# A bidirectional encoder layer: four staging tiles for streamed rows, and a transposed channel tile that stays in its accumulator

## The chip, the cores and the metric

The kernel runs on one core of a Trainium2 chip. The metric is the device time of one execution in microseconds (us); lower is better. The core's engines each run their own list of instructions in order: TensorE (PE) for matmuls and transposes, with its weight loads as a second row in the profile (PEld), VectorE (DVE), ScalarE (ACT) and GpSimd (POOL) for elementwise work, and SyncE (SP), which here only issues transfers (DMAs) from HBM to SBUF. POOL and ACT issue some DMAs too. Semaphores order the engines among each other.

## The reference

One layer over two batches with the same weights: a prompt P of 512 tokens and a sample S of 1024 tokens, 1024 channels. Cut to what matters here:

```python
proj = group_rmsnorm(h, norm_mix_pre) @ w_in
y_ssd, y_hy = ...                 # chunked state-space scan; long convolution
mix = concatenate([y_ssd, y_hy]) @ w_out            # 2048 -> 1024
h = h + group_rmsnorm(mix, norm_mix_post)
u = group_rmsnorm(h, norm_ffn_pre)
ff = (silu(u @ w_gate) * (u @ w_up)) @ w_down       # hidden width 2816
h = h + group_rmsnorm(ff, norm_ffn_post)
gate = sigmoid(group_rmsnorm(h, ple_norm_pre) @ w_ple_gate)
e = p_l @ w_ple_proj                                # 256 -> 1024
h = h + group_rmsnorm(gate * e, ple_norm_post)
```

All inputs and outputs are float32.

## The kernel before

**Matmuls.** Each float32 operand is split into a high part and a low part of a reduced format (`fp32r`): ACT copies with rounding (`split_ps`, L325), DVE or POOL subtracts (L326, L293). `mm3` (L301 to L303) then makes three matmuls: high by high, and the two mixed ones. Weights are loaded by SP into `wst` (L277) and split into `whi` and `wlo`.

**The end of the program**, from about 1640 us, is where the change acts; `build` writes it at L1441 and following. First P ends its FFN. Then S is done in two groups of 512 tokens:

- the out-projection of group 0 (`out_group`), its first half of 512 output channels together with P's post-FFN chain, then P's embedding gate (`ple`), then the second half;
- the out-projection of group 1 in two halves, with the normalisation chain of group 0 (`out_post`) between its steps; after it the chain of group 1 on its own (`rush`);
- S's embedding projection (`ple_proj`), whose results are stored in HBM as `e_s`;
- gate and up projections (`gate_up`), whose products are stored in HBM as `hid_s`;
- the down projection of both groups (`down_group`), with the post-FFN chain of group 0 in the steps of group 1;
- the embedding gates and the outputs.

**Streamed rows.** The out-projection (16 rows of 128 channels) and the down projection (22 rows) don't hold their left operand in SBUF. For each half, `streamed` loads one row of 128 channels x 512 tokens into a staging tile `mx` (SP, L1196; from `mix_s` or `hid_s`, 256 KB), and `split_ps` makes `mh` (ACT) and `ml` (DVE) of it. There are two `mx`, three `mh` and three `ml`. A load into a tile that was used before waits until the DVE subtraction has read it. `stream_gemm` takes two rows a step, for four token tiles: 2 x 4 x 3 = 24 matmuls of 128 x 512.

`mx` has other users. In `ple_proj` for S it holds the two loads of embedding rows per group (L1352, transposed at L1356) and eight evicted tiles per group (ACT, L1370), each stored to `e_s` at the following line. In the first job of `gate_up` it holds the sums of weights that DVE makes (L1227).

**The chains.** `post_steps` is a generator: for each of four token tiles of an accumulator `acc` it normalises (DVE, L1059), adds the residual row `t` (loaded by SP at L1050, added by DVE at L1060), normalises again back into `acc[t]` (L333), transposes it 128 x 128 at a time into a PSUM bank (L339), and splits the result. Two residual rows are loaded at the chain's start, the other two on the way. In `half`, one step of the chain is taken after each step of the matmuls.

**The channels of S.** For S's FFN the split goes by `Sums.take` instead. The gate and up projections there use a seven-product scheme for a 2 x 2 block matrix, so the tiles of tokens 0 and 1 are held until those of tokens 2 and 3 are there, and seven combinations of them are made and split (`bh`, `bl`). In the kernel before, ACT copies the transposed tile from PSUM to one of two tiles `stage` (L129), each 128 x 4 x 128. The tokens are taken in the order 0, 2, 1, 3, so that a held tile is used by the next token tile.

**Order.** The order on each engine is set by the framework when the program is built: it simulates the instructions by its own cost model and lists them by that, and the tile pools say when a tile comes free. A change in the number of tiles can so move instructions that the change does not name. `rush` and `post` run with raised priority.

Of the kernel before, what the change touches and what calls it, by code (L numbers as in the profile page):

```python
# [112 lines left out]
class Sums:  # L113
# [8 lines left out]
    def block(self, p):  # L122
        return [x[p - 1] for x in self.parts]

    def take(self, ps, k, t):
        K, nc = self.k, self.k.nc
        if t < 2:
            x = self.stage[t, k] = K.T(self.pool, [128, 4, 128], "stage")
            nc.scalar.activation(x, ps, AF.Copy)  # L129
            return  # L130
        c = slice((t - 2) * 128, (t - 1) * 128)

        def put(p, x):
            K.split_ps(x, *[z[:, :, c] for z in self.block(p)])

        def diff(out, a, b):
            nc.vector.tensor_tensor(out=out, in0=a, in1=b, op=ALU.subtract)

        b11, b21 = self.stage[t - 2, 0], self.stage[t - 2, 4]
        if k == 0:  # L140
            w = self.stage[t, 0] = K.T(self.pool, [128, 4, 128], "wsum")
            diff(w, ps, b11)
            put(1, b11)
            put(5, w)
            return
        w = self.stage[t, 0]
        put(3, ps)
        diff(w, ps, w)
        put(2, b21)
        put(6, w)  # L150
        diff(b11, w, b11)
        put(7, b11)
        diff(b21, b21, w)
        put(4, b21)
# [12 lines left out]
class Kern:  # L167
# [160 lines left out]
    def norm_tile(self, pool, src, dst, gain, u, t, wide=False, r=None):  # L328

        nc = self.nc  # L330
        if r is None:
            r = self.rstd(self.sumsq(pool, src), D)
        nc.vector.scalar_tensor_tensor(dst, src, r, gain, ALU.mult, ALU.mult)  # L333
        n = 8 if wide else 4
        for k in range(0, 8, n):
            ps = self.gps().rearrange("p a (k n) -> p (a k) n", k=4) if wide else \
                self.aps().rearrange("p (k n) -> p k n", k=4)
            for i in range(n):
                nc.tensor.transpose(ps[:, i], dst[:, (k + i) * 128:(k + i + 1) * 128], self.ident)  # L339
            if isinstance(u, Sums):  # L340
                u.take(ps, k, t)
            else:
                self.split_ps(ps, *u.put(k, n, t))

# [1052 lines left out]
    def build(self):  # L1397
# [40 lines left out]
        def tags(pool, *sizes):  # L1438
            return {t: (pool, t, n) for t, n in sizes}

        with self.pool("mix_s", side="right") as mp, ExitStack() as right:  # L1441
            pm = tags(mp, ("mx", 2), ("mh", 3), ("ml", 3))
            tr = right.enter_context(self.pool("out_s", side="right"))
            po = pm | tags(tr, ("acc", 4), ("row", 2), ("t4", 2), ("junk", 1), ("stage", 2), ("wsum", 1))
            with self.pool("tail_u") as tu, self.pool("tail_p") as tp:
                pl = tags(tu, ("et", 3), ("hh", 4), ("hl", 4), ("t4", 2), ("uh", 2), ("ul", 2))
                pl |= tags(tp, ("acc", 4), ("mst", 1), ("row", 2), ("junk", 1))
                pl["mx"] = pl["t4"]
                pl["ga"] = pl["acc"]
                mix = self.mix_in(P, 0, pl, 0, 8)  # L1450
                acc = self.new_acc(pl)
                self.outproj(P, 0, pl, acc, 0, mix)
                emb = self.ple_proj(pl, P, 0)
                next(emb)
                u = self.outproj(P, 0, pl, acc, 8, self.mix_in(P, 0, pl, 8, 8), lambda: self.new_u(pl, 4))
                next(emb)
                self.dma_lo = True
                u, chain = self.ffn(P, 0, pl, u)
                self.dma_lo = False
                acc = self.new_acc(po)  # L1460
                out = self.out_group(S, 0, po, acc)
                self.half(out, chain)
                self.ple_post(P, 0, pl, self.ple(P, 0, pl, u))
            self.apool = self.pools["x"][0]
            self.half(out)
            with self.pool("blocks") as tb:
                pb = pm | tags(tb, ("bh", 14), ("bl", 14))
                po |= pb
                u0, chain = self.out_post(S, 0, po, acc)
                acc = self.new_acc(po)  # L1470
                out = self.out_group(S, 1, po, acc)
                self.half(out, chain)
                self.half(out, chain)
                u1, chain = self.out_post(S, 1, po, acc)
                self.rush(chain)
                right.close()
                with self.pool("hid_s", side="right") as tr:
                    ph = pb | tags(tr, ("wsum", 3), ("sc", 5), ("gt", 6))
                    pe = pb | {"wsum": pm["mx"], "gt": pm["mh"], "sc": pm["ml"]}
                    pe |= {"et": pm["mx"], "hh": pm["mh"], "hl": pm["ml"]}  # L1480
                    self.apool = self.pools["m"][0]
                    for g in range(2):
                        for _ in self.ple_proj(pe, S, g):
                            pass
                    both = {0: u0, 1: u1}
                    self.gate_up(S, [(p, m, {g: both[g] for g in gs}) for p, gs, ms in (
                        (pe, [0], (0,)), (ph, [1], (0,)), (ph, [0, 1], range(2, NF, 2))) for m in ms], pe)
                with self.pool("end_s", side="right") as tr:
                    pe = pb | tags(tr, ("row", 3), ("t4", 3), ("junk", 1), ("mst", 2))
                    pe |= {"acc": pe["bl"], "ga": pe["bh"]}  # L1490
                    self.wide_tail = True
                    v0, chain = self.down_group(S, 0, pe)
                    v1, chain = self.down_group(S, 1, pe, chain)
                    self.rush(chain)
                    for g, v in ((0, v0), (1, v1)):
                        self.ple_post(S, g, pe, self.ple(S, g, pe, v))
# [30 lines left out]
```

## Time and profile before

| | |
|---|---|
| runs | 2855.67, 2855.22, 2851.17 us; median 2855.22 |
| profiled execution | 2852.23 us, span 2850.3 us |
| PE busy | 2683.8 us, 94% of the span |
| DVE, ACT, POOL busy | 1742.6, 1336.4, 1380.7 us |

How to read it: a row of groups gives line, engine, operation, destination<-sources, shape, count, then the busy time and the mean of one in ns, and then the idle time just ahead of these instructions with what ended it. A row of waits gives the engine and line that waited, what it waited for, the total in us, how often, and the longest. "SPq" is SP's DMA queue: the instruction at its head waits. PEclk is the clock that PE was granted, as a share of the full one. In the chain of waits each row has a start, a length and what took it.

### The profile page before, as it was taken

The page shows a single profiled execution, that of the slowest core. Times are in us where ns is not written, and L with a number is a line of the kernel's source. Part 1 is how long each engine was busy: PE and PEld are TensorE (multiplying, and loading weights), DVE is VectorE, ACT ScalarE, POOL GpSimd, SP SyncE. Part 2 cuts the span into 40 slices and gives each one's busy share as a digit, 9 for nine tenths or more (in the row PEclk, how much of TensorE's full clock was granted, in tenths as well). Part 3 has the DMA queues.
Part 4 walks back from the last instruction along what each step waited for, and adds up shares of the span by engine and source line. Part 5 has one row for each costly group of instructions (what it writes and reads, how often), then busy time and mean ns, then how long its engine had stood idle before and what let it go on. Part 6 is the DMA issues. An engine that isn't in the chain of part 4 may idle for free.

```text
span 2850.3 us, 41685 instructions
## 1 busy us (share of the span) xinstructions
PE 2683.8 (94%) x14696; PEld 2254.9 (79%) x14696; DVE 1742.6 (61%) x2893; ACT 1336.4 (47%) x2580; POOL 1380.7 (48%) x1137
## 2 busy tenths in 40 slices
PE   7999999999999989889999998987799999999998
PEld 5987888778888767578778776766699999877776
DVE  6767896977666896966676734475343444325345
ACT  4434445773234564745444454365533333344453
POOL 4445555443453556535444444554454444445464
PEclk9999999999999999989999999999999999999999
DMA  5544555744345576778888886565632222366665
GB/s 169 180 137 127 150 174 185 219 141 138 99 123 160 154 249 202 223 206 206 199 181 204 187 218 218 177 222 183 157 100 82 79 75 86 119 207 207 203 202 186
DMA packets 448507, 480.04 MB, mean 168 GB/s; under 512 B 29409, under 2 KB 330281, under 8 KB 445995
## 3 DMA queue, kind: packets, MB, share of 16 engines
q1 hardware_dynamic: 340923, 347.34, 40.0%
q0 software_dynamic: 28224, 68.17, 10.8%
q10 hardware_dynamic: 79152, 61.88, 6.9%
q8 instruction: 116, 1.90, 0.3%
q14 instruction: 92, 0.75, 0.1%
HBM read 346.54 MB, written 91.95 MB: 154 GB/s over the span
## 4 chain that ended last, share of the span: by engine, by line
PE 66%; DVE 15%; DMA 8%; issue 5%; POOL 3%; ACT 2%; SPq 0%; POOLq 0%; ACTq 0%; DVEq 0%
PE g L301 17%; PE g L303 16%; PE g L302 16%; PE a L302 3%; PE a L303 3%; PE a L301 3%; PE a L700 1%; DVE b L692 1%; DVE W L619 1%; DVE E L615 1%; PE a L973 1%; POOL wlo L293 1%; DMA wlo<-wst 1%; PE a L404 1%; DMA mx<-mix_s 1%
## 5 line engine op out<-in xcount | busy, mean ns | idle before, releaser
L293 POOL TENSOR_TENSOR wlo<-wst,whi 128x512 fp32r<-128x512 f32 (+1 forms) x544 | 786.1, 1452 | 756.6 <-ACT whi L292 691.5
L292 ACT ACTIVATE whi<-wst 128x512 fp32r<-128x512 f32 (+1 forms) x544 | 339.5, 628 | 532.9 <-PE g L302 330.0
L301 PE MATMUL g<-uh,whi 128*128 128x512 f32 (+1 forms) x1232 | 493.5, 401 | 8.5 <-DVE cv L393 4.4
L303 PE MATMUL g<-uh,wlo 128*128 128x512 f32 (+1 forms) x1232 | 491.6, 399 | 0.0
L302 PE MATMUL g<-ul,whi 128*128 128x512 f32 (+1 forms) x1232 | 490.9, 398 | 0.0
L301 PE MATMUL g<-bh,whi 128*128 128x256 f32 x1056 | 293.0, 283 | 14.3 <-ACT sc L1266 3.8
L303 PE MATMUL g<-bh,wlo 128*128 128x256 f32 x1056 | 294.0, 281 | 4.2 <-DMA wlo<-mx 2.7
L302 PE MATMUL g<-bl,whi 128*128 128x256 f32 x1056 | 294.3, 280 | 0.0
L301 PEld LDWEIGHTS g<-uh,whi 128*128 128x128 f32 x1232 | 233.2, 189 | 67.5 <-issue 10.4
L303 PEld LDWEIGHTS g<-uh,wlo 128*128 128x128 f32 x1232 | 232.6, 189 | 53.9 <-issue 5.8
L302 PEld LDWEIGHTS g<-ul,whi 128*128 128x128 f32 x1232 | 232.9, 189 | 53.4 <-issue 7.2
L326 DVE TENSOR_TENSOR ml<-mx,mh 128x512 fp32r<-128x512 f32 x152 | 122.4, 808 | 222.0 <-ACT mh L325 221.9
L285 POOL DMA_DIRECT2D wlo<-wst x144 | 126.0, 930 | 226.2 <-ACT wlo L284 211.1
L393 DVE SCALAR_TENSOR_TENSOR cv<-g,cols,cv 128x510 f32<-128x510 f32 (+3 forms) x192 | 193.0, 1006 | 64.9 <-ACT cv L387 62.8
L301 PEld LDWEIGHTS g<-bh,whi 128*128 128x128 f32 x1056 | 197.2, 189 | 20.0 <-DVE gt L1227 6.1
L303 PEld LDWEIGHTS g<-bh,wlo 128*128 128x128 f32 x1056 | 199.6, 189 | 4.9 <-DMA wlo<-mx 2.9
L302 PEld LDWEIGHTS g<-bl,whi 128*128 128x128 f32 x1056 | 199.5, 189 | 0.1
L301 PE MATMUL g<-whi,mh 128*128 128x512 f32 x412 | 169.7, 412 | 23.7 <-ACT mh L325 16.3
L302 PE MATMUL g<-wlo,uh 128*128 128x264 f32 (+1 forms) x576 | 191.3, 332 | 0.5 <-POOL wlo L293 0.5
L303 PE MATMUL g<-whi,ul 128*128 128x264 f32 (+1 forms) x576 | 189.9, 331 | 1.6 <-DVE rs_t L308 1.6
L309 POOL TENSOR_TENSOR rs_t<-rs_t,nhalf 128x1 f32<-128x1 f32 (+2 forms) x112 | 120.0, 1074 | 144.0 <-DVE rs_t L308 141.5
L301 PE MATMUL g<-whi,uh 128*128 128x264 f32 (+1 forms) x576 | 189.0, 330 | 0.0
(334 smaller groups left out, 6030.5 us busy)
## 6 DMA issues: line engine op xcount, KB each, us to landing
wst<-in_w_in SPq DMA_DIRECT2D x192, 256.0 KB
wlo<-wst POOLq DMA_DIRECT2D x144, 256.0 KB, 4.9
wst<-in_w_down SPq DMA_DIRECT2D x132, 256.0 KB
wst<-in_w_out SPq DMA_DIRECT2D x96, 256.0 KB
wst<-in_w_gate SPq DMA_DIRECT2D x92, 256.0 KB
wst<-in_w_up SPq DMA_DIRECT2D x92, 256.0 KB
mx<-hid_s SPq DMA_DIRECT2D x88, 256.0 KB
rw<-rows_s SPq DMA_DIRECT2D x32, 512.0 KB
```

Of the source, the lines that this page charges most:

```text
L285: nc.gpsimd.dma_start(lo, w, accum_op=ALU.add)
L292: nc.scalar.activation(hi, w, AF.Copy)
L293: (eng or nc.gpsimd).tensor_tensor(out=lo, in0=w, in1=hi.bitcast(F32), op=ALU.subtract)
L301: nc.tensor.matmul(ps, lh, rh, start=first, stop=False, skip_group_check=shared)
L302: nc.tensor.matmul(ps, lh, rl, start=False, stop=False, skip_group_check=shared)
L303: nc.tensor.matmul(ps, ll, rh, start=False, stop=last, skip_group_check=shared)
L309: nc.gpsimd.tensor_tensor(out=t[:, :w], in0=t[:, :w], in1=self.nhalf[:, :w], op=ALU.pow)
L326: self.nc.vector.tensor_tensor(out=lo, in0=ps, in1=hi.bitcast(F32), op=ALU.subtract)
L393: nc.vector.scalar_tensor_tensor(out[:, a:b], ps[:, a + d:b + d], wcol(w), out[:, a:b], ALU.mult, ALU.add)
L404: nc.tensor.transpose(ps[:, j * 128:(j + 1) * 128], srcs[i + j], self.ident)
L615: nc.vector.scalar_tensor_tensor(E[:, h], rw[:, 0, h], dbf[:, c, gh:gh + 1], rw[:, 1, h], ALU.add, ALU.min)
L619: nc.vector.scalar_tensor_tensor(W[:, h], su, dt[:, c, gh:gh + 1], W[:, h], ALU.mult, ALU.add)
```

## The change

`mx` gets four tiles in place of two (L1442), and the pool `stage` goes (L1444). With the two stages left out, the SBUF used is the same: two tiles of 128 x 512 float32 less and two more. `Sums.take` is given the source tile `dst`, that is `acc[t]`, and for tokens 0 and 1 ACT copies the transposed tile back into the 512 columns of `acc[t]` from which it came. The later differences and splits read and overwrite it there. No other line changes, and the number of instructions on each engine is the same.

```diff
-    def take(self, ps, k, t):
+    def take(self, ps, k, t, src):
+
         K, nc = self.k, self.k.nc
         if t < 2:
-            x = self.stage[t, k] = K.T(self.pool, [128, 4, 128], "stage")
+            x = self.stage[t, k] = src[:, k * 128:(k + 4) * 128].rearrange("p (k n) -> p k n", k=4)
             nc.scalar.activation(x, ps, AF.Copy)
             return
...
             if isinstance(u, Sums):
-                u.take(ps, k, t)
+                u.take(ps, k, t, dst)
...
-            pm = tags(mp, ("mx", 2), ("mh", 3), ("ml", 3))
+            pm = tags(mp, ("mx", 4), ("mh", 3), ("ml", 3))
...
-            po = pm | tags(tr, ("acc", 4), ("row", 2), ("t4", 2), ("junk", 1), ("stage", 2), ("wsum", 1))
+            po = pm | tags(tr, ("acc", 4), ("row", 2), ("t4", 2), ("junk", 1), ("wsum", 1))
```

The order before S's first out-projection is as it was; from there it differs. After the change line numbers from L125 on are one higher. In the rows below, a number behind a name tells one tile from another.

First place, term (f): SP's queue late in `gate_up`, with the first loads of the down projection's rows (`mx` from `hid_s`) among the weight loads. Before:

```order
L277 DMA wst_20916<-in_w_gate 128x4x128
L1196 DMA mx_24285<-hid_s 128x512
L277 DMA wst_20918<-in_w_gate 128x4x128
L277 DMA wst_21141<-in_w_up 128x4x128
L277 DMA wst_21143<-in_w_up 128x4x128
L277 DMA wst_21145<-in_w_up 128x4x128
L277 DMA wst_21147<-in_w_up 128x4x128
L277 DMA wst_21370<-in_w_gate 128x4x128
```

After the change, at the same place:

```order
L278 DMA wst_20908<-in_w_gate 128x4x128
L1197 DMA mx_24277<-hid_s 128x512
L1197 DMA mx_24283<-hid_s 128x512
L278 DMA wst_20910<-in_w_gate 128x4x128
L278 DMA wst_21133<-in_w_up 128x4x128
L278 DMA wst_21135<-in_w_up 128x4x128
L278 DMA wst_21137<-in_w_up 128x4x128
L278 DMA wst_21139<-in_w_up 128x4x128
L278 DMA wst_21362<-in_w_gate 128x4x128
L278 DMA wst_21364<-in_w_gate 128x4x128
L278 DMA wst_21366<-in_w_gate 128x4x128
L1197 DMA mx_24325<-hid_s 128x512
```

A second and a third row are moved here, ahead of weight loads that they stood behind.

Second place, term (b): PE in the first half of S's first out-projection (`g` is its PSUM), with the transposes of P's post-FFN chain (`a`). Before:

```order
L303 MATMUL g_16329<-whi_16629,ml_16618 128x512
L339 MATMUL a_16599<-ident_105,acc_13502 128x128 x4
L339 MATMUL a_16606<-ident_105,acc_13502 128x128 x4
L301 MATMUL g_16328<-whi_16635,mh_16623 128x512
L302 MATMUL g_16328<-wlo_16636,mh_16623 128x512
```

After the change, around the first of the same two batches of four transposes:

```order
L302 MATMUL g_16328<-whi_16701,mh_16689 128x512
L303 MATMUL g_16328<-wlo_16702,mh_16689 128x512
L340 MATMUL a_16599<-ident_105,acc_13502 128x128 x4
L304 MATMUL g_16328<-whi_16701,ml_16690 128x512
L303 MATMUL g_16329<-wlo_16702,mh_16689 128x512
L304 MATMUL g_16329<-whi_16701,ml_16690 128x512
```

and around the second, whose first row here is the 25th behind the first batch:

```order
L302 MATMUL g_16329<-whi_16764,mh_16752 128x512
L303 MATMUL g_16329<-wlo_16765,mh_16752 128x512
L340 MATMUL a_16606<-ident_105,acc_13502 128x128 x4
L304 MATMUL g_16329<-whi_16764,ml_16753 128x512
L302 MATMUL g_16329<-whi_16764,mh_16752 128x512
```

The two batches stood back to back and have 26 matmuls between them now; both come later among the matmuls.

Third place, the new cost: SP's queue in the first half of S's second out-projection, with the residual rows of the chain of group 0 (`t` from `in_x_sample`). Before:

```order
L1196 DMA mx_17854<-mix_s 128x512
L277 DMA wst_18153<-in_w_out 128x512
L1050 DMA t_3575_17846<-in_x_sample 128x1024
L1196 DMA mx_17937<-mix_s 128x512
L277 DMA wst_18203<-in_w_out 128x512
L1050 DMA t_3594_17935<-in_x_sample 128x1024
```

After the change:

```order
L1197 DMA mx_17935<-mix_s 128x512
L1197 DMA mx_17941<-mix_s 128x512
L1197 DMA mx_18005<-mix_s 128x512
L278 DMA wst_18149<-in_w_out 128x512
L1051 DMA t_3573_17844<-in_x_sample 128x1024
L1197 DMA mx_18011<-mix_s 128x512
L278 DMA wst_18199<-in_w_out 128x512
L1051 DMA t_3592_17933<-in_x_sample 128x1024
```

The first residual row stood behind the streamed row `mx_17854`; now it stands behind the three rows that follow that one (the first of them was `mx_17937` and is `mx_17935` here). The second stands three streamed rows later as well, behind `mx_18011` where it was behind `mx_17937`.

## Prediction

> **What bounds the kernel now.** First the page: the busy shares and the chain of work that ended last.
>
> ```profile
> span 2850.3 us, 41685 instructions
> PE 2683.8 (94%) x14696; PEld 2254.9 (79%) x14696; DVE 1742.6 (61%) x2893; ACT 1336.4 (47%) x2580; POOL 1380.7 (48%) x1137
> PE 66%; DVE 15%; DMA 8%; issue 5%; POOL 3%; ACT 2%; SPq 0%; POOLq 0%; ACTq 0%; DVEq 0%
> ```
>
> TensorE (PE) is busy for 94% of the span and the change leaves it every matmul, so only its idle time and its slow-clock time can move. The staging tiles `mx` are used from about 1640 us on. The second view is therefore the table of stretches there; its columns are the stretch, its length, then PE, weight loads, DVE, ACT and POOL busy time (instructions), the granted PE clock, DMA share and GB/s.
>
> ```profile
> 1698.00:1757.00 59.00, 50.57 (x226) 38.90 (x225) 37.77 (x41) 29.53 (x53) 33.69 (x29) 1.00 0.77 255
> 1801.00:1855.00 54.00, 47.54 (x200) 36.73 (x199) 33.19 (x30) 25.09 (x45) 33.26 (x27) 1.00 0.65 214
> 1855.00:1915.00 60.00, 50.79 (x220) 38.90 (x219) 49.95 (x57) 37.27 (x69) 32.37 (x28) 0.97 0.68 224
> 1959.00:2012.00 53.00, 36.25 (x146) 24.86 (x145) 35.08 (x50) 33.23 (x65) 17.18 (x17) 0.84 0.47 159
> 2012.00:2060.00 48.00, 37.62 (x279) 35.48 (x278) 18.93 (x29) 29.16 (x58) 26.69 (x25) 0.93 0.78 179
> 2460.00:2500.00 40.00, 33.31 (x191) 27.90 (x189) 8.65 (x10) 11.23 (x20) 16.02 (x13) 0.99 0.59 198
> 2500.00:2530.00 30.00, 29.66 (x116) 23.78 (x117) 9.85 (x12) 11.93 (x21) 11.34 (x9) 0.90 0.59 187
> 2595.00:2660.00 65.00, 58.36 (x248) 45.41 (x247) 41.39 (x45) 34.62 (x64) 35.57 (x31) 0.95 0.66 222
> 2660.00:2760.00 100.00, 100.00 (x431) 80.62 (x430) 35.13 (x44) 48.29 (x86) 51.71 (x42) 1.00 0.55 174
> ```
>
> The last row is the undisturbed pace: 100 / 431 = 0.232 us for a matmul, and 5.57 us for the 24 that two streamed rows feed (2 rows x 4 token tiles x 3). In the other eight PE idles 8.43 + 6.46 + 9.21 + 16.75 + 10.38 + 6.69 + 0.34 + 6.64 = 64.9 us. That is the most there is, clock aside.
>
> Third, what PE waited for there (total us, times, longest), in the order 1698 to 1757, 1801 to 1855, 1855 to 1915, 1959 to 2012, 2480 to 2504, 2595 to 2660:
>
> ```profile
> PE a L339 <- DVE ul L326: 4.2, 4, 1.5
> PE g L301 <- ACT mh L325: 2.6, 2, 1.9
> PE g L303 <- DVE ml L326: 1.6, 3, 0.8
> ...
> PE a L303 <- DVE ml L326: 4.2, 4, 1.4
> PE a L301 <- ACT mh L325: 2.2, 2, 1.3
> ...
> PE g L301 <- ACT mh L325: 3.6, 3, 1.4
> PE g L303 <- DVE rs_t L308: 2.2, 1, 2.2
> ...
> PE g L301 <- ACT mx L1370: 6.7, 5, 4.0
> PE a L1356 <- DMA mx<-in_p_sample: 3.5, 1, 3.5
> ...
> PE g L301 <- ACT mh L325: 5.1, 3, 3.4
> ...
> PE g L303 <- DVE ml L326: 4.5, 3, 1.8
> PE g L301 <- ACT mh L325: 1.8, 1, 1.8
> ```
>
> `mh` and `ml` are the split of a streamed row, so PE mostly waits for rows. Whether ACT and DVE are late themselves, or their input `mx` is, the fourth view says: ACT's groups between 1500 and 2850 us, and the chain of waits in the second half of S's first out-projection (start, us, what).
>
> ```profile
> L325 ACT ACTIVATE mh<-mx 128x512 fp32r<-128x512 f32 x152 | 95.5, 629 | 179.5 <-PE g L302 85.9 <-DMA mx<-mix_s 44.8 <-DMA mx<-hid_s 43.9
> ```
>
> ```profile
> 1827.92 5.45 DMA mx<-mix_s
> ...
> 1833.45 0.64 ACT mh L325
> ...
> 1834.12 0.70 DVE ml L326
> ...
> 1834.83 3.58 DMA mx<-mix_s
> ...
> 1839.88 4.51 DMA mx<-mix_s
> ...
> 1845.87 2.55 DMA mx<-mix_s
> ...
> 1849.88 2.60 DMA mx<-mix_s
> ```
>
> ACT idles 88.7 us for loads of `mx`. The chain shows the loop: load, split on ACT, split on DVE, and only then the next load, for it needs the tile that DVE has just read. Four rounds take (1849.88 - 1827.92) = 21.96 us, 5.49 each; each tile brings one row a round, so two tiles bring two rows in 5.49 us where PE needs 5.57. There is no reserve: any delay of DVE or SP reaches PE. Four tiles allow 11.1 us a round.
>
> **The change part by part.** The counts of instructions stay the same on every engine. The copy to `stage` (ACT, L129) becomes a copy of the same size to `acc`: 0, as nothing is added. `acc` is held longer, until its tile of the same column is used; that is in the new cost below. Everything else is order.
>
> (a) P's last FFN projection: the order before it is the same. 0.
>
> (b) 1698 to 1757, the first out-projection half under P's FFN chain: 4.2 + 2.6 + 1.6 = 8.4 us. The transposes (L339) wait since two batches of four stand back to back and share one PSUM bank; in the new order 26 matmuls, 26 x 0.232 = 6.0 us, lie between them, more than the longest wait of 1.5. With the `mh` wait of 2.6 gone as well it could be 6.8; since the batches that now fall later can meet P's gate projection, I take 5.5 (0 to 8.4).
>
> (c) 1801 to 1855: 4.2 + 2.2 = 6.4. Here the rows are late because DVE is, as well as the loads:
>
> ```profile
> 1821.52 2.85 DVE L1059 SCALAR_TENSOR_TENSOR acc<-acc,rs_t,row 128x1024 f32<-128x1024 f32 x1
> ```
>
> One such operation ahead of a split costs 2.85 us whatever the number of tiles, but only three `mh` stand in reserve of it. I take 2.5 (0 to 6.4).
>
> (d) 1855 to 1915: PE idles 9.21, but DVE is busy for 49.95 of 60 us. I take 2 (0 to 9.2).
>
> (e) 1959 to 2060. `mx` here also holds S's embedding rows and the sixteen evicted tiles of the embedding projection, each held until its store has landed, and then the first weight sums of the gate projection. The third load of rows now waits for store 5 of the first group instead of 7, and the first sum for store 13 of 16 instead of 15:
>
> ```profile
> DVE mx L1227 <- DMA e_s<-mx: 13.0, 2, 11.2
> ```
>
> The 3.5 us of L1356 should go. The 4.0 us wait on L1370 stays, for ACT evicts as late as before. Of the 11.2 that DVE waits I let 4.5 reach PE, less than half, as it has idle time of 10.38 us right behind (row 2012 to 2060). Sum 8 (3.5 to 3.5 + 11.2 = 14.7).
>
> (f) 2480 to 2530, the start of the down projection: 5.1 us for `mh`, since the third row's load stands behind weight loads in SP's queue, and ACT splits it only here:
>
> ```profile
> 2489.83 0.63 ACT L325 ACTIVATE mh<-mx 128x512 fp32r<-128x512 f32 x1 [5.62 <-DMA mx<-hid_s]
> ```
>
> Now seven rows (4 `mx` + 3 `mh`) can stand ready and not five, and two loads move ahead. The wait of 3.4 is followed by a slow clock: in 2500 to 2530 the 116 matmuls took 29.66, at the pace 116 x 0.232 = 26.9, so 2.8 more. 5.1 + 2.8 = 7.9, 8 taken (5.1 to 8).
>
> (g) 2595 to 2660: 4.5 + 1.8 = 6.3 under S's FFN chain, with DVE as in (c). I take 1 (0 to 6.6).
>
> **New cost.** The residual rows of each chain (`t`, L1050) share SP's queue with `mx`. Its loads of `mx` wait, before (first 1860 to 1960, then 2480 to 2770):
>
> ```profile
> SPq L1196 <- DVE ml L326: 27.0, 23, 2.4
> ...
> SPq L1196 <- DVE ml L326: 94.9, 74, 6.5
> ```
>
> With more `mx` loads ahead, each of the two late loads of `t` may come later; the mean wait is 27.0 / 23 = 1.2 us. One such wait for two late loads in two chains is 4 x 1.2 = 4.8, so -5. It can be 0. At the worst two `mx` loads more stand ahead of each, at their longest: 2 x 2 x 2.4 in S's second out-projection and 2 x 6.5 in the down projection, -22.6.
>
> Sum: 5.5 + 2.5 + 2 + 8 + 8 + 1 - 5 = 22 us. The profiled execution took 2852.2 (span 2850.3 and 1.9 around it), so 2830; the median of the runs, 2855.2, is 3.0 above it, and with these the forecast is 2833.
>
> **Rivals.** *Two tiles already suffice* and the waits come from ACT's and DVE's order. For it: (c), (d) and (g) lie under chains that fill DVE, and the last two loads above took only 2.55 and 2.60 us. Against it: the other three took 5.45, 3.58 and 4.51, and 88.7 us of ACT's idle time ended with such a load. Then only (f) without the clock and L1356 go: 5.1 + 3.5 = 8.6, and 2852.2 - 8.6 + 3.0 = 2847.
>
> The Trainium skill, page "DMA: Bandwidth & Descriptors", section "Anatomy of one DMA — SWDGE (gpsimd) path", speaks for this rival: a transfer costs 2.0 us and its bytes over 436 GB/s. For the 256 KB of a row that is an estimate of 2.60 us, and a round of 2.60 + 0.64 + 0.70 = 3.94, well under 5.57. Two of the five loads here agree, three do not (mean of the five 3.74); the page's figure comes from another queue, and the measurement decides.
>
> *Late residual rows: slower.* More `mx` loads before `t` in SP's first-in-first-out queue, each waiting for DVE; DVE waits in turn for `t`, and all splits behind that wait stop, so SP stops too. For it: a load of `t` already stands in the chain of waits.
>
> ```profile
> 1876.52 6.78 DMA t<-in_x_sample
> ```
>
> Against it: an `mx` load waits for DVE less often when four tiles stand. At the worst price it is 22.6 less the 8.6 of the first rival, 14 slower, 2852.2 + 14 + 3.0 = 2869. It decides once it costs more than those 8.6 and the 5.7 that can be told (below), 14.3.
>
> *Nearly all goes*: (b) 8.4, (c) 6.4, (d) half, 4.6, (e) 14.7, (f) 8, (g) half, 3.3: sum 45, and 2852.2 - 45 + 3.0 = 2810. For it: a deep queue takes up the 2.85 us of DVE in (c) as well. Against it: `mh` and `ml` remain at three.
>
> That the change does nothing is excluded by the moved loads, and little of it would be the first rival.
>
> **How the numbers follow.** A measurement of this kernel can tell about 0.2%, 5.7 us, from no change: faster is under 2849.5, slower over 2860.9. The forecast has 0.52, two tiles suffice 0.24 (a little under half of it, 0.11, would be faster and 0.13 within 0.2%), late rows 0.14, nearly all 0.10. Faster 0.52 + 0.10 + 0.11 = 0.73, the same 0.13, slower 0.14. The range goes from the largest gain, 2810, to 2858, which holds the first rival and the milder part of late rows.
>
> **What the profile after would show.** Right: ACT's 44.8 and 43.9 us of idle time for `mx` are under half; no `mh` wait over 1 us where the down projection starts, and a clock of 1.00 in the 30 us after it; L1356 no longer waits for its load; the transposes wait under 1.5 us in (b). Wrong: PE idle in the eight stretches that falls by less than 10 us with the ACT waits gone (then DVE's order was the bound); a wait of DVE L1060 for `t` longer than 6.78, or new ones in the down projection (late rows).

## The result, and the profile after

| | before | after the change |
|---|---|---|
| median of 6 runs each | 2854.37 us (2851.17 to 2855.67) | 2840.79 us (2836.93 to 2843.63) |
| span of the profiled execution | 2850.3 us | 2838.2 us |

The ratio is 0.9949, with a 95% interval of 0.9938 to 0.9961. By the medians it is 13.6 us less, clear of the 0.2% that can be told. The forecast was 22 us less, 2833, in a range of 2810 to 2858. So the direction was right, the time lies in the range, and the gain was about six tenths of the forecast. That is not because every term came out at six tenths. Some came as forecast, some were much larger, and some were losses where the forecast had none.

The page of the change: span, busy shares and the chain that ended last.

```profile
span 2838.2 us, 41732 instructions
PE 2687.0 (95%) x14696; PEld 2261.8 (80%) x14696; DVE 1763.3 (62%) x2893; ACT 1333.0 (47%) x2580; POOL 1383.5 (49%) x1137
PE 71%; DVE 14%; DMA 5%; issue 4%; POOL 3%; ACT 2%; SPq 0%; POOLq 0%; DVEq 0%; ACTq 0%
```

The chain of waits goes through PE for 71% in place of 66%, and through DMAs for 5% in place of 8%. The first thing that the prediction named is there: ACT's idle time ahead of a row's split that a load of `mx` ended was 44.8 + 43.9 = 88.7 us. The same group of the change, between 1500 and 2850 us:

```profile
L326 ACT ACTIVATE mh<-mx 128x512 fp32r<-128x512 f32 x152 | 95.8, 630 | 190.8 <-PE g L303 157.3 <-DMA mx<-hid_s 17.9 <-DMA mx<-mix_s 9.1
```

It is 27.0 us now, and ACT mostly waits for a free `mh`, that is for PE. (This sign is weaker than it looks: with three tiles, e7 below, this idle time is 60.2 us, more than half of 88.7, and the gain is all there.) The second thing is there too: the start of the down projection in the table of stretches (the stretch, its length, PE busy and so on as in the prediction, the clock third from the right).

```profile
2460.00:2500.00 40.00, 38.09 (x221) 32.97 (x220) 12.71 (x13) 12.95 (x23) 18.88 (x14) 1.00 0.53 181
2500.00:2530.00 30.00, 30.00 (x130) 24.12 (x129) 8.02 (x11) 12.92 (x23) 14.60 (x11) 1.00 0.78 258
2595.00:2660.00 65.00, 60.92 (x271) 48.84 (x270) 45.67 (x48) 36.56 (x68) 38.83 (x32) 0.97 0.73 240
```

PE idles 1.91 us in the first where it had 6.69, and the clock stays at 1.00 in the second where it had 0.90.

To see where the 12.1 us between the two spans lie, the stages must be measured by themselves, since they begin at other times now. The next table gives for each stage the time from the start of its first matmul to that of the next stage, read from the timeline of PE. The rows for the start of the down projection, before and after, show how:

```profile
2479.01 0.50 PE L301 MATMUL g<-whi,mh 128*128 128x512 f32 x1 [0.78 <-DVE sc L1227]
2544.99 0.40 PE L301 MATMUL a<-whi,mh 128*128 128x512 f32 x1
```

```profile
2480.62 0.50 PE L302 MATMUL g<-whi,mh 128*128 128x512 f32 x1 [0.78 <-DVE sc L1228]
2538.19 0.40 PE L302 MATMUL a<-whi,mh 128*128 128x512 f32 x1
```

2544.99 - 2479.01 = 66.0 us, and 2538.19 - 2480.62 = 57.6.

| stage | before | change | difference | forecast |
|---|---|---|---|---|
| (a) P's last FFN projection | 24.9 | 29.8 | +4.9 | 0 |
| (b) S's first out-projection, first half | 58.9 | 54.5 | -4.5 | -5.5 |
| P's gate projection | 44.4 | 46.2 | +1.8 | not in the sum |
| (c) S's first out-projection, second half, to its last token tile | 51.7 | 53.7 | +2.0 | -2.5 |
| (d) from there to the end of the first half of S's second | 62.2 | 58.5 | -3.7 | -2 |
| second half of S's second | 42.9 | 43.0 | 0 | 0 |
| (e) S's last chain and embedding projection, to the first gate matmul | 53.6 | 51.5 | -2.1 | -8, with the gate's start |
| gate and up projections | 467.5 | 468.0 | +0.5 | |
| (f) down projection, first half | 66.0 | 57.6 | -8.4 | -8 |
| second half | 60.1 | 60.1 | 0 | 0 |
| (g) third half | 78.2 | 72.8 | -5.4 | -1 |
| the rest | 155.7 | 155.8 | +0.1 | 0 |

The forecast had a further +5 for the new cost, without a stage. The sum of the differences is -14.8, and the change's execution was 2.4 us later than the other when it came to (a), in a part where the order is the same: -12.4, against -12.1 by the spans.

Two cautions. Each stage is read from one execution, so differences of a few us in a long stage mean little: in e10, which is the change once more, the gate and up projections took 465.8 us and not 468.0, and over these runs (e4 aside) stage (a) begins anywhere from 1669.4 to 1676.6 us. And a boundary doesn't always cut at the same matmul: (b) has 225 PE instructions before and 218 after, and P's gate projection 193 and 203, since two of the chain's eight batches of four transposes moved from the one to the other.

Three lines need an explanation: the losses in (a) and (c), and the gain in (g).

**(a)** What P's last FFN projection waited for in the change, and the chain of waits ahead of it (start, us, what):

```profile
PE g L303 <- DMA wlo<-wst: 3.5, 2, 2.7
PE g L302 <- ACT whi L287: 1.3, 1, 1.3
```

```profile
1660.53 3.20 DMA mix_s<-b
1663.82 1.42 DMA mx<-mix_s
...
1675.71 13.96 DMA wst<-in_w_down
```

PE waits for weights. Their last load was issued at 1675.71 and took 13.96 us. Ahead of it SP has the streamed rows, and the first of them could only start at 1663.82, behind the last store of S's long convolution (`mix_s<-b`). In SP's timeline before, the first row's load went out 22 us earlier, and the last two weight loads followed one another from 1670.02:

```profile
1641.75 0.34 SPq L1196 DMA_DIRECT2D mx<-mix_s  x1
...
1670.02 1.86 SPq L277 DMA_DIRECT2D wst<-in_w_down  x2
```

The first row of `mix_s` doesn't come from the long convolution. It is proposed that the store matters since the pool of the staging tiles is 4 KB larger in each partition and now reaches into the memory of `b`; this is a theory until it is tested (e5).

**(c)** One of DVE's and one of PE's waits in the second half of S's first out-projection (1805 to 1864):

```profile
DVE t L1061 <- DMA t<-h_p: 6.6, 1, 6.6
```

```profile
PE a L304 <- DVE ml L327: 6.4, 5, 2.8
```

The timelines of DVE, of POOL and of SP's queue there:

```profile
1841.13 1.23 DVE L1061 TENSOR_TENSOR t<-acc,t 128x1024 f32<-128x1024 f32 x1 [6.63 <-DMA t<-h_p]
1842.28 7.72 DVE L327 TENSOR_TENSOR ml<-mx,mh 128x512 fp32r<-128x512 f32 x4
```

```profile
1843.25 4.99 POOL L294 TENSOR_TENSOR wlo<-wst,whi 128x512 fp32r<-128x512 f32 x4
```

```profile
1826.97 6.68 SPq L1197 DMA_DIRECT2D mx<-mix_s  x3
...
1834.18 0.42 SPq L1051 DMA_DIRECT2D t<-h_p  x1
```

This is the rival of late residual rows, in a chain that the prediction had not thought of: P's last one (`ple_post`). SP issues three streamed rows, which wait for splits, ahead of the fourth residual row. That goes out 1834.18 - 1805.86 = 28.3 us after the start of the stage, where it was 25.8 before, and DVE can use it at 1841.13. DVE stands for 6.63 us (1.9 before), four splits pile up behind it, and PE waits 2.79 for one of them.

**(g)** is read with the prediction's own step below.

### The profile page after: what moved, and what is told of

Its sections match the earlier page's. It is cut to its first block, busy times and chain, and to the rows that moved or that the text cites. A ratio compares the mean times of both kernels' runs of the same rounds, so it can differ in the third digit from the quotient of the medians.

```text
span 2838.2 us, 41732 instructions
## 1 busy us (share of the span) xinstructions
PE 2687.0 (95%) x14696; PEld 2261.8 (80%) x14696; DVE 1763.3 (62%) x2893; ACT 1333.0 (47%) x2580; POOL 1383.5 (49%) x1137
## 3 DMA queue, kind: packets, MB, share of 16 engines
q0 software_dynamic: 28224, 68.17, 10.8%
## 4 chain that ended last, share of the span: by engine, by line
PE 71%; DVE 14%; DMA 5%; issue 4%; POOL 3%; ACT 2%; SPq 0%; POOLq 0%; DVEq 0%; ACTq 0%
PE g L302 18%; PE g L304 18%; PE g L303 18%; PE a L304 3%; PE a L303 3%; PE a L302 3%; PE a L701 1%; DVE W L620 1%; PE a L974 1%; DVE E L616 1%; DVE b L693 1%; POOL wlo L294 1%; PE a L405 1%; DVE ml L327 1%; PE a L629 1%
## 5 line engine op out<-in xcount | busy, mean ns | idle before, releaser
L327 DVE TENSOR_TENSOR ml<-mx,mh 128x512 fp32r<-128x512 f32 x152 | 141.8, 941 | 183.5 <-ACT mh L326 180.2
L326 ACT ACTIVATE mh<-mx 128x512 fp32r<-128x512 f32 x152 | 95.8, 630 | 190.8 <-PE g L303 157.3
```

The costliest lines, as they stand in the source:

```text
L326: self.nc.scalar.activation(hi, ps, AF.Copy)
L327: self.nc.vector.tensor_tensor(out=lo, in0=ps, in1=hi.bitcast(F32), op=ALU.subtract)
```

## The experiments

Each is the change with one edit (e8, e9 and e12 with more, as said there; e10 with none), and is timed against the kernel before on the same chip. Ratios are given to the kernel before, with 95% intervals; the change itself has 0.9949. Stage times are read as in the table.

### e1: two tiles, with the copy to the accumulator kept

```diff
-            pm = tags(mp, ("mx", 4), ("mh", 3), ("ml", 3))
+            pm = tags(mp, ("mx", 2), ("mh", 3), ("ml", 3))
```

> The change with two staging tiles again; the transposed tiles still stay in the accumulator. Theory (the gain comes from the depth of the staged rows): the time of before within 3 us, a ratio of 0.999 to 1.001, and the start of the down projection waits for its rows as before. Rival (the accumulator copy reorders the chains, and the gain is theirs): the time of the change, a ratio of 0.995.

Measured: 2858.85 us, a ratio of 1.0019 (1.0007 to 1.0030), 5.4 us more than before. The rival falls: the copy brings nothing. But the theory's 0.999 to 1.001 was missed on the other side: the copy costs something. The start of the down projection takes 65.3 us and the third half 78.1, as before (66.0, 78.2). The loss lies in S's last chain with the embedding projection, 56.9 against 53.6, and a smaller one in the first half of S's first out-projection, 60.4 against 58.9. PE's waits in the former (1957 to 2017):

```profile
PE g L302 <- ACT mx L1371: 6.1, 3, 4.7
PE a L1357 <- DMA mx<-in_p_sample: 4.8, 1, 4.8
...
PE a L340 <- DVE acc L334: 2.3, 2, 1.2
```

The waits that were there before are longer (L1357 had 3.5, the longest on L1371 was 4.0), and the transposes wait for DVE's normalised `acc` for 2.3 us, which they did not. So the depth of the staging tiles is worth about 13.6 + 5.4 = 19 us, and the copy takes 5.4 of it (the 5.4 by the ratio).

### e2 and e3: four tiles on one side only

In both there are two `mx`, and a second tag `my` of two tiles is taken in turn with them. e2 has it for the down projection alone, in the pool that opens when the gate and up projections end:

```diff
-            pm = tags(mp, ("mx", 4), ("mh", 3), ("ml", 3))
+            pm = tags(mp, ("mx", 2), ("mh", 3), ("ml", 3))
...
                     pe = pb | tags(tr, ("row", 3), ("t4", 3), ("junk", 1), ("mst", 2))
+                    pe["mx"] = [pm["mx"], (tr, "my", 2)]
```

e3 has it up to the end of the gate and up projections, and the down projection has `first`:

```diff
-            pm = tags(mp, ("mx", 4), ("mh", 3), ("ml", 3))
+            pm = tags(mp, ("mx", 2), ("my", 2), ("mh", 3), ("ml", 3))
+            first = pm["mx"]
+            pm["mx"] = [first, pm["my"]]
...
                     pe = pb | tags(tr, ("row", 3), ("t4", 3), ("junk", 1), ("mst", 2))
+                    pe["mx"] = first
```

> Four staging tiles in the down projection alone, two before it; the accumulator copy stays. Theory (what the two profiles show): the start of the down projection gains 8.4 us and its third half 5.4, and the loss of 4.9 in P's last FFN projection does not come, so 13.8 us less than before, a ratio of 0.9952. Rival (the split of the gain in the prediction, where the down projection has 9 of 27): 4.5 us less, 0.9984.

> Four staging tiles up to the gate and up projections, two in the down projection. Theory (the two profiles): the stages up to there sum to -1.0 us (+4.9 -4.5 +1.8 +2.6 -4.3 -2.0 +0.5), so a ratio of 0.9996, and the down projection as before. Rival (the prediction's split, 18 of 27 less 5): 13 us less, 0.9955.

Measured: e2 2855.46 us, a ratio of 0.9996 (0.9986 to 1.0006); e3 2852.83 us, 0.9997 (0.9984 to 1.0009). e3 came out at the number that the two profiles gave: up to the gate projection, four tiles and the copy balance each other. The stages of its one profile can't confirm this. That execution is the fastest of the run, 10 us under its median, and up to the end of the gate and up projections it is 4.9 us under the kernel before and not 1.0, as S's last chain with the embedding projection took 47.6 us (51.5 in the change). Why is open.

e2 missed. Its third half takes 72.4 us, the whole of the 5.4 gained. But the first half takes 69.8 in place of 57.6. The splits there, and SP's issue of the rows:

```profile
DVE ml L331 <- DMA my<-hid_s: 7.3, 1, 7.3
```

```profile
2492.55 0.80 SPq L1201 DMA_DIRECT2D my<-hid_s  x2
2497.37 0.33 SPq L1201 DMA_DIRECT2D my<-hid_s  x1
```

The two added tiles lie in a pool whose memory the gate and up projections hold to their end, so the second row can't be loaded until 2492.55. In the change the first rows are loaded among the weights of those projections. So (f) isn't the number of tiles in the down projection. It is that they are free before it starts. And as the first half lost 3.8 and S's last chain with the embedding projection 4.3 (57.9 us, as in e1), the ratio says nothing against the theory on the third.

### e4: four residual tiles for P's last chain

```diff
-                  tags=("bh", "bl", "bl", "bh") if last else ("t4",) * 4)
+                  tags=("bh", "bl", "bl", "bh") if last else ("t4", "t5", "t4", "t5") if q is self.P else ("t4",) * 4)
...
-                pl |= tags(tp, ("acc", 4), ("mst", 1), ("row", 2), ("junk", 1))
+                pl |= tags(tp, ("acc", 4), ("mst", 1), ("row", 2), ("junk", 1), ("t5", 2))
```

> The change, and P's last chain has four tiles for its residual rows in place of two, so that all four are loaded in P's gate projection and none stands between streamed rows. Theory (the second half of S's first out-projection lost 2.6 us because VectorE waited 6.6 us for a late residual row): that wait goes, the half takes 54 us or less in place of 57.3, and the time is 3 to 5 us under the change, a ratio to before of 0.9936. Rival (VectorE's own order is the limit there): as the change, 0.9951.

Measured: 2911.1 us, a ratio of 1.0189 (1.0162 to 1.0216), 54 us more by the ratio. Yet the stage that it was made for did what the theory said: 47.7 us in place of 53.7, to its last token tile as in the table (the expectation's 57.3 counts on to the next half). The 54 us were lost hundreds of us earlier. The table of stretches, of the change and then of e4, and one of SP's waits in e4 between 900 and 1200:

```profile
800.00:1200.00 400.00, 386.09 (x1783) 301.21 (x1781) 308.99 (x547) 207.98 (x493) 208.91 (x156) 0.97 0.59 181
1200.00:1400.00 200.00, 181.89 (x927) 149.89 (x928) 134.72 (x233) 99.33 (x190) 89.08 (x75) 0.95 0.85 211
```

```profile
800.00:1200.00 400.00, 348.94 (x1534) 264.42 (x1533) 293.76 (x554) 193.53 (x480) 177.12 (x133) 0.89 0.53 163
1200.00:1400.00 200.00, 158.90 (x846) 134.13 (x845) 148.06 (x214) 76.92 (x127) 97.29 (x67) 0.91 0.60 172
```

```profile
SPq L322 <- DMA mix_s<-mt: 19.6, 1, 19.6
```

PE idles 51.1 + 41.1 us there in place of 13.9 + 18.1, 60 us more. In that part P's tail is woven into S's scan. SP's queue stands 19.6 us at the load of a gain row (L322), a tile of the pool that was made 8 KB larger, until a store of S's scan has read its own tile (`mt`); in the change none of SP's seven largest waits in that stretch is of this kind. It is a wait of the kind proposed for (a), a larger pool that meets memory still in use, at a much worse place. How much of the 60 us this wait makes, and which tiles overlap, is not shown.

### e5: the staging tiles on top

```diff
-        with self.pool("mix_s", side="right") as mp, ExitStack() as right:
-            pm = tags(mp, ("mx", 4), ("mh", 3), ("ml", 3))
+        with self.pool("mx_s", side="right") as xp, self.pool("mix_s", side="right") as mp, ExitStack() as right:
+            pm = tags(xp, ("mx", 4)) | tags(mp, ("mh", 3), ("ml", 3))
```

> The change, with the four staging tiles in a pool of their own opened ahead of that of the splits, so that they lie higher in SBUF and the splits lie where the staging tiles would be. Theory (P's last FFN projection lost 4.9 us because the larger pool reaches into the memory of P's long convolution, and the first staged row waits for its last store, so that seven rows meet the last weight loads): the first row is loaded 20 us earlier and that projection takes 27 us or less in place of 29.8, the time is 3 to 5 us under the change, a ratio of 0.9936. Rival (the loads of the last weights are late by their place in the queue alone): as the change, 0.9951.

Measured: 2832.45 us, a ratio of 0.9938 (0.9920 to 0.9956). SP's first row in e5:

```profile
1645.45 0.34 SPq L1197 DMA_DIRECT2D mx<-mix_s  x1
```

It goes out 18 us earlier than in the change, with the same number of tiles and no other edit than their place. P's last FFN projection takes 26.9 us in place of 29.8, and PE's wait for `wlo` falls from 3.5 to 2.1. So the place in SBUF made the first load late, and that made 2.9 of the 4.9 us. What the other 2.0 are, the stretches of this stage say, before, in the change, in e5 and in e8 below, which has the same place and the same loads in SP's queue:

```profile
1672.88:1697.77 24.89, 22.75 (x98) 17.79 (x97) 7.94 (x12) 9.54 (x17) 6.82 (x7) 1.00 0.76 209
1675.32:1705.15 29.83, 25.05 (x98) 19.47 (x96) 7.93 (x12) 9.64 (x17) 7.16 (x8) 0.89 0.71 207
1676.55:1703.44 26.89, 24.83 (x98) 18.77 (x96) 7.93 (x12) 9.54 (x17) 6.82 (x7) 0.94 0.72 197
1670.39:1695.37 24.98, 22.71 (x98) 17.79 (x96) 7.93 (x12) 9.54 (x17) 6.81 (x7) 1.00 0.76 205
```

PE idles 2.14, 4.78, 2.06 and 2.27 us. The 4.9 us were 2.6 of idle time and 2.3 of slow clock. With the new place all of the added idle time is gone; the 2.0 that stay in e5 are slow clock alone (0.94), which e8 doesn't have. e2 has it as well, with two tiles and the loads in the old order (26.2 us at 0.93). The rival falls: the last two weight loads keep their place behind three rows and a residual row in e5 and e8, and PE waits about as long as in the kernel before. Of the whole, 0.9938 and 0.9949 can't be told apart: S's last chain with the embedding projection took 53.9 where the change had 51.5, and gate and up 465.9 where it had 468.0 (and 465.8 in e10).

### e6: the residual row in a tile that is free

```diff
-                  tags=("bh", "bl", "bl", "bh") if last else ("t4",) * 4)
+                  tags=("bh", "bl", "bl", "bh") if last else ("t4", "row", "t4", "t4") if q is self.P else ("t4",) * 4)
```

> The change, with the third residual row of P's last chain in the free tile of the gain rows, so that the fourth is loaded where the third was, without a larger pool. Theory (VectorE waited 6.6 us for that fourth row): the wait goes, the second half of S's first out-projection takes 54 us or less in place of 57.3 between its first matmul and the next half, and the time is 3 to 5 us under the change, a ratio to before of 0.9936. Rival (VectorE's order is the limit): as the change, 0.9951.

Measured: 2834.09 us, a ratio of 0.9944 (0.9924 to 0.9964). DVE no longer waits for a residual row in that half, and it takes 47.7 us in place of 53.7, 6.0 less (51.7 before). What PE still waits for there:

```profile
PE a L304 <- DVE ml L327: 2.6, 3, 1.0
```

The theory holds for the stage, and its rival falls there: DVE's order was not the limit. The time moved the right way, but the interval holds the change's 0.9949 as well.

### e7: three tiles

```diff
-            pm = tags(mp, ("mx", 4), ("mh", 3), ("ml", 3))
+            pm = tags(mp, ("mx", 3), ("mh", 3), ("ml", 3))
```

> The change with three staging tiles. Theory (a round of load and splits took 5.49 us of the 5.57 that two rows may take, and a third tile allows 8.2): most of the gain in the third half of the down projection, 5.4, comes with the third tile, and half of the 8.4 at its start; against two tiles with the accumulator copy that is 10 us or more less, a ratio to before of 0.9985 or less. Rival (the gain is the number of rows that stand ready, the same for each tile): half of the 19 us between two and four tiles, a ratio of 0.9984 with half in each place.

Measured: 2829.73 us, a ratio of 0.9929 (0.9909 to 0.9949). Three tiles are at least as good as four. The third half of the down projection takes 73.0 us (72.8 with four tiles, 78.1 with two), its start 57.8 (57.6 and 65.3). So the third tile gives all of both gains, where the theory had half at the start and the rival had half in each. The second half of S's first out-projection takes 48.1 us against 53.7: with one tile less, fewer streamed rows stand ahead of the residual row, and DVE waits for it 3.7 us in place of 6.6.

```profile
DVE t L1061 <- DMA t<-h_p: 3.7, 1, 3.7
```

### e8: e5 and e6 together

> The change with both of the edits before: the staging tiles on top, and the residual row in the free tile. Theory: the two add up, 6 to 10 us under the change, a ratio to before of 0.992. Rival: what one stage gains, the next gives back; as the change, 0.9951.

Measured: 2830.5 us, a ratio of 0.9924 (0.9903 to 0.9944). P's last FFN projection takes 25.0 us and the second half of S's first out-projection 47.7: the two stages add up, 4.8 + 6.0 = 10.8 us, 1.9 of it the slow clock that e5 still had. S's last chain with the embedding projection took 53.8, 2.3 more, as in e5. By the ratios that is 7 us under the change, within the 6 to 10 that were expected, though the intervals overlap.

### e9: two tiles for the embedding projection

Four tiles for the streamed rows as in e3, here in the down projection too, and for the embedding projection and the first weight sums only `first`:

```diff
-                    pe = pb | {"wsum": pm["mx"], "gt": pm["mh"], "sc": pm["ml"]}
-                    pe |= {"et": pm["mx"], "hh": pm["mh"], "hl": pm["ml"]}
+                    pe = pb | {"wsum": first, "gt": pm["mh"], "sc": pm["ml"]}
+                    pe |= {"et": first, "hh": pm["mh"], "hl": pm["ml"]}
```

> The change, with two of the four staging tiles for S's embedding projection and the first weight sums, four for the streamed rows. Theory (the embedding projection gains by four tiles what it lost by the accumulator copy): from the last streamed row to the first gate matmul 56.9 us, as with two tiles, in place of 51.5, and 5 us over the change, a ratio to before of 0.9968. Rival (ScalarE's and VectorE's order sets that stretch): 51.5 us and the time of the change, 0.9951.

Measured: 2840.83 us, a ratio of 0.9949 (0.9934 to 0.9965), with the change itself at 0.9934 on that chip (e10). The stage takes 56.6 us against 51.4, as the theory had it (56.9, 51.5); the 3.6 us between the medians are of that size, but the intervals overlap. So four tiles were worth 5.2 us in (e), and the copy had taken 3.3 of these.

### e10 to e12: the change and three tiles again, and three tiles on top

e12 is e7 with the pool of e5.

> The change as it stands, beside its variants on one chip. Four tiles should lie 5.6 us above three by the second half of S's first out-projection (53.7 us in place of 48.1): a ratio to before of 0.9949.

> Three staging tiles again, beside four on one chip. Theory (the third tile gives the reserve, the fourth only sends rows ahead of a residual row): 5.6 us under the change, a ratio to before of 0.9929. Rival (the difference was the spread of the runs): as the change, 0.9949.

> Three staging tiles, in a pool of their own on top of that of the splits. Theory: the 2.9 us that P's last FFN projection gained by the placement with four tiles come with three too, and S's embedding projection gives up to 2.4 back; 0.5 to 3 us under three tiles, a ratio to before of 0.9925.

Measured on one chip: the change 2837.22 us, 0.9934 (0.9918 to 0.9950); three tiles 2832.04, 0.9920 (0.9900 to 0.9940); three on top 2828.78, 0.9900 (0.9880 to 0.9920). The second half of S's first out-projection took 52.8, 48.2 and 47.4 us. That three tiles are not worse than four is shown twice; that they are better is shown for the stage, while the two intervals of the time overlap. e12 has the lowest ratio of all, and its interval reaches just into that of the change: P's last FFN projection took 27.2 us (29.3 in e10), and S's last chain with the embedding projection 53.8 (51.4). It is the version to take from here, about 25 us under the kernel before.

## Why the prediction was right, and where it was not

**The bound** was read rightly. "There is no reserve": a round of load and splits took 5.49 us of the 5.57 that two rows may take, and two tiles bring two rows a round. If that is so, a third tile (8.2 us for a round) is all that is needed, and e7 shows just this. The first rival, that two tiles suffice, falls with e1: with two tiles hardly anything of (f) and (g) comes (0.7 and 0.1 us), with three all of it. Still, the sign that was named for the bound, ACT's idle time for `mx` under half, is not what the gain hangs on: with three tiles it is 31.3 + 28.9 = 60.2 of 88.7 us, and PE no longer feels it.

**(f), 8 forecast, 8.4 measured**: the wait and the slow clock behind it went, both by their numbers. e2 adds that the tiles must be free while the gate and up projections run, which is what the moved loads in SP's queue had shown.

**(b), 5.5 forecast, 4.5 measured**, came close by luck. The transposes no longer wait for the one PSUM bank (4.2 us before, in four waits), as the step said. But the first batch now waits for the normalised accumulator (1700 to 1765), against the sign that they would wait under 1.5 us:

```profile
PE a L340 <- DVE acc L334: 3.4, 1, 3.4
```

So the transposes gave 0.8 us, and the `mh` wait of 2.6, which the step held only for possible, went whole. The waits fell from 8.4 to 5.0. The last 1.0 is work that moved: PE was busy 50.51 us (225 instructions) and is busy 49.48 (218), and two batches of transposes stand in P's gate projection now, which took 1.8 us more. The two stages together gained 2.7.

**(g), 1 forecast, 5.4 measured** was mis-sized. The step said that DVE's order set the 6.3 us of waits there. With more tiles the waits fell to 4.1 us:

```profile
PE g L304 <- DVE ml L327: 4.1, 2, 2.2
```

The waits before were 6.6 with the small one on `rs_t`, so 2.5 went. The rest is the clock, which the step left out although its row showed 0.95. The third half as a whole, before and after:

```profile
2605.05:2683.27 78.22, 71.58 (x304) 56.03 (x303) 44.86 (x50) 40.78 (x75) 40.98 (x34) 0.96 0.66 218
2598.25:2671.04 72.79, 68.72 (x304) 55.04 (x303) 47.13 (x50) 40.31 (x75) 41.43 (x34) 0.98 0.72 235
```

PE idled 6.64 us and idles 4.07, and for the same 304 instructions it was busy 71.58 and is busy 68.72: 2.6 + 2.9 = 5.4 us with rounding. The same clock term was counted in (f).

**(c) and (d)**, 2.5 and 2 forecast, were of the right kind and too small: without the late residual row (e6) they are 51.7 - 47.7 = 4.0 and 62.2 - 59.0 = 3.2 (the boundary between them moves by four matmuls, 0.9 us; together they are 7.2). "One such operation ahead of a split costs 2.85 us whatever the number of tiles" was too strict.

**The new cost, 5 forecast, 6.0 measured** (e6): right in mechanism, wrong in place, and its size is luck. It was put in the chains of S, as four waits of 1.2 us. All waits of DVE for residual rows of S's chains grew only from 4.0 to 5.7 us (1.1 for one in S's second out-projection). The 6.0 came in P's last chain, from a single row: DVE's wait grew by 4.7 us, the splits behind it piled up, and a slow clock followed. The sign for it, a wait of DVE over 6.78 us, was set too high: 6.78 is the length of a load, where the longest such wait of DVE before was 3.0 us, and the 6.6 that came stayed just under it.

**(e), 8 forecast, 2.1 measured, is the step that failed most.** The L1356 wait of 3.5 us is gone, but behind the transposes a wait of 2.32 us for `mh` came in its place, while ACT makes splits of the last chain (all waits for `mh` in this stage: 3.2 us before, 5.1 after):

```profile
1998.12 0.50 PE L302 MATMUL g<-whi,mh 128*128 128x512 f32 x1 [2.32 <-ACT mh L326]
```

The 4.5 us that were to come from the earlier weight sums can't be seen on PE: DVE's wait for the stores fell from 13.0 to 7.5 us, but in the first 48.4 us of the gate projection PE idles 10.2 us where it idled 10.4, as it waits 5.8 us for ACT's split of weights where it waited 3.8. (Gate and up took 0.5 us more here and 1.7 less in e10, so up to 2 us may be hidden.) And the copy took 3.3 of what the tiles gave (e1, e9).

**"The copy to `stage` becomes a copy of the same size to `acc`: 0"** was wrong: it costs 5.4 us with two tiles (e1; 2.0 to 8.6 by its interval). The work is the same, as the prediction said, but the chain is ordered differently, as the waits of e1 show. Why the order costs this is open, and no run has four tiles together with the old `stage`, so the cost of the copy is known with two tiles only.

**"(a): the order before it is the same. 0"** was wrong by 4.9 us. The order of PE's work there is the same, but not that of SP's loads. The place of the pool made the first row late and the last weights with it, which gave 2.6 us of idle time; the other 2.3 are slow clock (e5, e8).

So the sum came out 13.6 of 22 because errors of opposite signs partly cancelled: (a) -4.9, (e) -6 and (b) with P's gate -2.8, against (g) +4.4; the errors of the other terms are under 2 us each. That it lies in the range so owes something to luck.

## What to carry to other kernels

When a load goes into a tile that its reader has just left, compare the length of one round with the time that the consumer needs for what a round brings: if the two are about equal, one more buffer removes the wait, and a second more may only put loads ahead of something that a slower engine needs. A pool that grows also moves: look up what else lived in the memory that it now covers, and when that is free, for a load can wait there for a stage with which it has nothing to do. And price a wait together with the clock behind it.

## What the runs showed of the hardware

**A slow clock can follow a wait under 3 us.** The rows of PE in the change behind the 2.79 us wait in (c):

```profile
1848.85 0.73 PE L304 MATMUL a<-whi,ml 128*128 128x512 f32 x1 [2.79 <-DVE ml L327]
1849.38 0.63 PE L302 MATMUL a<-whi,mh 128*128 128x512 f32 x1
1849.80 0.63 PE L303 MATMUL a<-wlo,mh 128*128 128x512 f32 x1
...
1852.36 0.40 PE L303 MATMUL g<-wlo,mh 128*128 128x512 f32 x1
1852.60 0.40 PE L304 MATMUL g<-whi,ml 128*128 128x512 f32 x1
```

The matmuls start 0.42 us apart until 1852.36, 3.5 us after the wait, and then 0.24. The Trainium skill, page "TensorE: Matmul & The Clock Gate", section "What's actually happening", has PE at half clock after at least one idle window of about 3.4 us, and back at the full one after about 3.4 us of work. The way back agrees (3.5 us). The way down does not: 2.79 us of idle time were enough here, with one of 1.02 us five us ahead. The wait alone doesn't decide it: in e10 the wait at this place was 2.75 us, and PE went on at 0.23 us a matmul for 1.3 us before it slowed for 3.4 us; and in (a) two waits of 1.56 and 0.27 us, close together, were followed by 3.4 us at the slow pace in e5, while two of 1.97 and 0.30 at the same place in e8 were not.

**DVE's splits got longer.** The mean of `ml` (L327) rose from 808 to 941 ns, 122.4 to 141.8 us in all. In the rows of (c), four splits took 7.72 us beside four subtractions of POOL (4.99 us). Four at the 0.69 us of an undisturbed one and these 4.99 are 7.75, so they seem to have taken turns. The Trainium skill, page "SBUF — State Buffer", section "SBUF: two separate sides", has a port pair that DVE (with two inputs in SBUF) and GpSimd hold in turn for a whole instruction; the sum agrees, but no run here tested it. The two profiles point the same way: of the splits that stand alone in the timeline between 1640 and 2850 us, the 37 that overlap no instruction of POOL took at most 0.70 us, and every longer one (up to 2.3 us but for one of 4.77) overlaps one.

```profile
L327 DVE TENSOR_TENSOR ml<-mx,mh 128x512 fp32r<-128x512 f32 x152 | 141.8, 941 | 183.5 <-ACT mh L326 180.2 <-PE g L304 3.0
```
